# Values turned to token rows at the end of their projection, the bonus per token and head, in one layer of a hybrid backbone

## The chip, the cores and the metric

The kernel runs on one core of a Trainium2 chip, as one launch. The metric is the device time of a run in microseconds. Three runs of the kernel before took 1710.25 to 1720.92 us, median 1714.06; the profiled execution took 1717.3, and its trace spans 1715.5.

## The reference

One layer: 512 latent tokens and 256 context tokens of width 2048 are normalised, modulated and projected by one input matrix. Group A (16 heads of 64) is a state recurrence in two directions; each direction starts from the final state of the context's scan. Group B (16 query heads on 4 key heads) is windowed attention with all context keys. Both are gated, and projected by one output matrix. The part that the change is about:

```python
def _rwkv_output(y, prep, r_k, ln_g, ln_b):
    r, v, _, _, _, kd = prep
    mu = jnp.mean(y, axis=-1, keepdims=True)
    var = jnp.mean(jnp.square(y - mu), axis=-1, keepdims=True)
    yn = ((y - mu) * lax.rsqrt(var + GN_EPS)).reshape(B, L, RWKV_WIDTH) * ln_g + ln_b
    bonus = jnp.einsum('blhn,bldhn,hn->blh', r, kd, r_k)[..., None] * v
    return yn + bonus.reshape(B, L, RWKV_WIDTH)
```

The bonus is one number for each token and head, times that token's 64 values of the head; `kd` is summed over the two directions. `v` is also what the recurrence writes into its state, and there it is wanted with tokens on partitions; `r`, `k` and the normalised output are worked on with channels on partitions.

## The kernel before

Everything is float32. The large products (input and output projection) are split in three float32r products of high and low halves. A weight part (128 input rows times 4, 128 columns) is loaded to a tile `wf`, halved by ScalarE and VectorE to `whi` and `wlo`, and used by 12 matmuls with 512 columns. These are called filler here.

No instruction is issued where the program text stands. The text is recorded as a list of operations with their dependences; `order` (line 430) plays them through with a duration for each and writes one fixed sequence per engine: operations of the recurrence and attention go by the length of the path behind them, and filler products go where no such operation is ready. All are then issued by line 497, which is why every row of the profile has that line; tiles tell operations apart. A tile name stands for a slot in a ring of buffers, which several tensors share: `kv` holds keys and values of a pair, `g` scratch, `p` the tensors of a latent pair and of its output (`r`, `kds`, `bv`, `h`), `uv` the values in token rows in the scan, `kon` constants (identity, the ones of the heads).

The stages, with their times in the trace:

- 0 to 226 us: normalisation and the first eight column tiles of the projection together (`lockstep`), among them the values of pairs 0, 1 and 2.
- 226 to 690: eight context units (segment 0), one for each pair of heads, with 14 further column tiles as filler, of 512 latent and 256 context columns each. The latent accumulators are two banks (`pl`), the context accumulator one (`pc`).
- 650 to 1361: eight pairs, each with two latent units (segments 1 and 2, the two directions). A unit goes through `pair` (once for both), `prep`, `stacks`, `relay_out`, `solve`, `levels` and `scan`; the second unit ends in `rwkv_out`, which normalises, adds the bonus, gates and stores `dmix`. Filler are the remaining input tiles (receptance, gates, queries), and then the first quarter of the output projection.
- 1280 to 1414: norms and rotary of queries and keys; the last input tiles. The loads of `dmix` into `xl`, `q` and `rz` serve the output projection.
- 1414 to 1580: attention, with output projection as filler; then output projection alone to the end.

Of the values, `evac` (985) stores a projected column tile by channel to `dv`. `pair` (1039) loads it to `kv`, turns it by two or four transposes (`pv`, in a bank of the ring `pt`), copies it to a `g` slot and stores it as token rows to `vt`; `scan` loads it from there to `uv`. The bonus is made in `stacks` (1158): `rr = r * r_k * kds`, then one product with a block of ones, 128x512, which gives each channel the sum of its head, then VectorE's product with the values of `kv` into `bv`. `bv` has one buffer; it takes the normalised output in `rwkv_out` (1379), is gated in place and is the source of the store of `dmix`. `h` is a ring of two.

Of the kernel before, what the change touches and what calls it, by code (L numbers as in the profile page):

```python
# [16 lines left out]
ALU = mybir.AluOpType  # L17
# [5 lines left out]
L = 512  # L23
C = 256
T = L + C
# [34 lines left out]
NLOCK = 4  # L60
# [114 lines left out]
s ssq:8 rsq0:8 rsq1:8 gmu:8 gvar:8 rso0:8 rso1:8 pc:8*4 sc4:8 ms4:16 xtmp:80 smid:128 mf:128 invx:128 ur:128 sm:128*2  # L175
"""
CTX = BOTH + """
x xi:256*2 qt:256 wga:512 | kv k:256 v:256 kk:256 | kr0 kr:1024 | kr1 kr:1024 | kr2 sh:768 gsel:4 | kk gsum:512
# [7 lines left out]
kv k:512 v:512 | kk kk:512 | p r:512 kds:512 bv:512 h:512*2 | sh sh:512  # L186
# [323 lines left out]
class Body:  # L510
# [61 lines left out]
    def setup(self):  # L572
        nc, a = self.nc, self.a
# [8 lines left out]
        o = 0  # L582
        c = constants()
# [13 lines left out]
        v = nc.vector  # L597
# [7 lines left out]
        d = self.dram  # L605
        self.dk = [self.t(d, (128, T), f"dk{p}") for p in range(8)]
        self.dv = [self.t(d, (128, T), f"dv{p}") for p in range(8)]
# [144 lines left out]
    def lockstep(self):  # L752
        nc, a = self.nc, self.a
        lp = self.lp = self.pool(LOCK)
# [18 lines left out]
        ada, mod, xs, wts, raw = {}, {}, {}, {}, []  # L773
        accl = [self.t(pp, (128, 512), f"accl{j}") for j in range(NLOCK)]
        accc = [self.t(pp, (128, 512), f"accc{j}") for j in range(NLOCK // 2)]
        accc = [accc[j // 2][:, 256 * (j % 2):256 * (j % 2) + 256] for j in range(NLOCK)]
# [127 lines left out]
        for c in range(2 * KC):  # L904
# [16 lines left out]
            if c == KC - 1:  # L921
                for j in range(NLOCK):
                    x = self.t(lp, (128, T), "raw")
# [8 lines left out]
        for j in range(NLOCK):  # L932
            for i in range(2):
                nc.tensor.matmul(pb[:, 4 * j + 2 * i:4 * j + 2 * i + 2], lhsT=acb[i][:, 128 * j:128 * j + 128],
                                 rhs=ones, start=True, stop=True)
        nc.vector.tensor_copy(bias.rearrange("p j i -> p (j i)"), pb[:, ::2])
        for j, x in enumerate(raw):
            for i, (o, n, *_) in enumerate(streams):
                nc.scalar.activation(x[:, o:o + n], x[:, o:o + n], AF.Identity, bias=bias[:, j, i:i + 1])
            self.evac(NLOCK + j, x[:, :L], x[:, L:], self.t(lp, (128, T), "xs"))  # L940
# [44 lines left out]
    def evac(self, j, pl, pc, o=None):  # L985
        nc = self.nc
        kind, i, _ = COLS[j]
# [27 lines left out]
        dst = {"k": self.dk, "v": self.dv, "ak": self.dak, "av": self.dav, "q": self.dq, "r": self.dr,  # L1015
               "zr": self.dzr, "za": self.dza}[kind][i]
        n = T if pc is not None else L
# [21 lines left out]
    def pair(self, s, p, wk, ps, lat):  # L1039
        nc = self.nc  # L1040
        n, off = (L, 0) if lat else (C, L)
        ntt = n // 128
# [4 lines left out]
        s.v = self.t(wk, (128, n), "v")  # L1047
        nc.sync.dma_start(out=s.v, in_=self.dv[p][:, off:off + n])
        self.n += 1
        s.vt = self.t(self.dram, (n, 128), f"vt{self.n}")  # L1050
# [24 lines left out]
        pv = self.t(ps, (128, 512), "pt", nm="pv")[:, :n]  # L1075
        for t in range(ntt):
            nc.tensor.transpose(pv[:, 128 * t:128 * t + 128], s.v[:, 128 * t:128 * t + 128], self.ident)
        vt = gen("vt")[:, :n]
        nc.scalar.copy(vt, pv)
        nc.sync.dma_start(out=s.vt.rearrange("(t q) c -> q t c", q=128), in_=vt.rearrange("q (t c) -> q t c", c=128))  # L1080
# [77 lines left out]
    def stacks(self, s, wk, ps):  # L1158
# [43 lines left out]
        if seg == 2:  # L1202
            rr = self.t(wk, (128, 512), "g", nm="rr")
            nc.vector.scalar_tensor_tensor(rr, pr.r, self.par["r_k"][:, p:p + 1], pr.kds, ALU.mult, ALU.mult)
            pb_ = pt("pbon")
            nc.tensor.matmul(pb_, lhsT=self.kon["bones"], rhs=rr, start=True, stop=True)
            pr.bv = self.t(wk, (128, 512), "bv")
            nc.vector.tensor_tensor(pr.bv, pb_, pr.v, ALU.mult)
# [170 lines left out]
    def rwkv_out(self, p, s, wk, ps):  # L1379

        nc = self.nc
        gen = lambda nm: self.t(wk, (128, 512), "h", bufs=2, nm=nm)
# [20 lines left out]
        nc.gpsimd.tensor_tensor(s.bv, o, s.bv, ALU.add)  # L1403
        o = s.bv
        self.gate(o, self.dzr[p], gen("gz"), gen("gth"))
# [296 lines left out]
```

## Time and profile before

| | |
|---|---|
| median of three runs | 1714.06 us (1710.25 to 1720.92) |
| profiled execution | 1717.3 us |
| its span | 1715.5 us |
| TensorE busy | 1570.0 us, 92% |
| weight loads busy | 1213.2 us, 71% |
| VectorE busy | 1342.5 us, 78% |
| ScalarE, GpSimd busy | 705.5 and 403.9 us |
| moved by DMA | 232.99 MB, mean 136 GB/s |
| mean granted clock of TensorE | 0.97 |

Times count from the start of the span. PE is TensorE, PEld its weight loads, DVE VectorE, ACT ScalarE, POOL GpSimd, SPq the queue of DMA issues. Matmuls overlap one another, so the busy times of single ones add up to more than the time that they take; the distance between two starts is what one costs. "Clock" is the share of full speed that TensorE was granted. A wait is put down to the releaser that came last.

### The profile page before, as it was taken

Reading aid. Unit: us, or ns where it says so; the run is one execution under the profiler, and the core shown is the slowest. Engines: PE = TensorE matmul, PEld = TensorE weight load, DVE = VectorE, ACT = ScalarE, POOL = GpSimd, SP = SyncE. Lnnn points to the kernel's source line nnn. Section 1 sums busy time; section 2 is a strip of 40 time slices with the busy share of each in tenths; the row PEclk is TensorE's granted clock in tenths of the full one; section 3 lists DMA queues with packets and bytes.
Section 4 is the critical chain, followed back from the end, with each engine's and each line's share of the span. In section 5 each row is a group of like instructions: output and inputs, shape, how many; then the busy total and the mean of one; then the engine's idle time right before and its main releaser. Section 6 shows DMA issues by size and latency. Waiting matters only on the chain.

```text
span 1715.5 us, 34198 instructions
## 1 busy us (share of the span) xinstructions
PE 1570.0 (92%) x12374; PEld 1213.2 (71%) x12374; DVE 1342.5 (78%) x3913; ACT 705.5 (41%) x1460; POOL 403.9 (24%) x615
## 2 busy tenths in 40 slices
PE   7998888999999999988899999899988979999998
PEld 4666777776777777766676676667765658787886
DVE  2457888887989646878789778887888877989965
ACT  3432363333334223433343334343433437777733
POOL 2358621110111002122223121222223350202000
PEclk9999999999999999989999999999998999999999
DMA  9976465534545433433343334243433363122136
GB/s 348 325 252 209 129 185 153 148 103 136 156 132 167 143 112 122 129 84 111 89 128 99 109 99 132 78 118 95 125 105 110 120 203 115 64 67 68 50 124 189
DMA packets 218122, 232.99 MB, mean 136 GB/s; under 512 B 79584, under 2 KB 140384, under 8 KB 217952
## 3 DMA queue, kind: packets, MB, share of 16 engines
q1 hardware_dynamic: 217952, 230.80, 43.7%
q8 instruction: 97, 1.59, 0.4%
q14 instruction: 73, 0.60, 0.1%
HBM read 194.55 MB, written 36.18 MB: 134 GB/s over the span
## 4 chain that ended last, share of the span: by engine, by line
PE 29%; DVE 23%; DMA 7%; issue 3%; ACT 1%; SPq 1%; POOL 0%; DVEq 0%; ACTq 0%; POOLq 0%
PE psum L497 29%; DVE x L497 7%; DVE s L497 5%; DVE e L497 2%; DMA x<-iw 2%; DVE ar L497 2%; DVE wlo.1_45_339 L497 2%; DVE wlo.0_42_301 L497 1%; SPq L497 1%; DMA iw<-x 1%; DVE bk L497 1%; DVE p L497 1%; DVE uv L497 1%; DMA nb<-it 1%; DMA wf.0_40_246<-in_wo_dram 1%
## 5 line engine op out<-in xcount | busy, mean ns | idle before, releaser
L497 PE MATMUL psum<-xh,whi.0_41_297 128*128 128x512 f32 x624 | 244.9, 415 | 1.2 <-ACT xh L497 0.5
L497 PE MATMUL psum<-xh,whi.1_44_327 128*128 128x512 f32 x624 | 240.3, 408 | 0.7 <-ACT xh L497 0.7
L497 PE MATMUL psum<-xh,wlo.1_45_339 128*128 128x512 f32 x528 | 218.2, 413 | 5.7 <-DVE wlo.1_45_339 L497 5.7
L497 PE MATMUL psum<-xh,wlo.0_42_301 128*128 128x512 f32 x528 | 215.8, 409 | 2.6 <-DVE wlo.0_42_301 L497 2.6
L497 PE MATMUL psum<-xl,whi.0_41_297 128*128 128x512 f32 x432 | 178.1, 412 | 5.8 <-DVE xl L497 5.8
L497 PE MATMUL psum<-xl,whi.1_44_327 128*128 128x512 f32 x432 | 177.4, 411 | 0.7 <-DVE xl L497 0.6
L497 DVE TENSOR_TENSOR s<-x,nb 128x60 f32<-128x60 f32 (+21 forms) x648 | 158.5, 245 | 10.0
L497 DVE TENSOR_TENSOR x<-x,s 128x60 f32<-128x60 f32 (+21 forms) x648 | 155.4, 240 | 10.6
L497 PEld LDWEIGHTS psum<-xh,whi.0_41_297 128*128 128x128 f32 x624 | 119.1, 193 | 30.1 <-issue 4.5
L497 PEld LDWEIGHTS psum<-xh,whi.1_44_327 128*128 128x128 f32 x624 | 118.7, 191 | 25.4 <-issue 2.3
L497 PEld LDWEIGHTS psum<-xh,wlo.1_45_339 128*128 128x128 f32 x528 | 101.7, 193 | 29.3 <-DVE wlo.1_45_339 L497 7.9
L497 PEld LDWEIGHTS psum<-xh,wlo.0_42_301 128*128 128x128 f32 x528 | 100.8, 191 | 25.7 <-DVE wlo.0_42_301 L497 4.2
L497 PEld LDWEIGHTS psum<-xl,whi.0_41_297 128*128 128x128 f32 x432 | 83.2, 193 | 26.1 <-DVE xl L497 7.5
L497 PEld LDWEIGHTS psum<-xl,whi.1_44_327 128*128 128x128 f32 x432 | 83.2, 193 | 17.9 <-DVE xl L497 1.5
L497 PE MATMUL psum<-kr,bk 64*128 64x128 f32 (+1 forms) x640 | 70.5, 305 | 20.1 <-DVE x L497 6.3
L497 PEld LDWEIGHTS psum<-kr,bk 64*128 64x128 f32 (+1 forms) x640 | 56.4, 201 | 36.8 <-issue 9.3
L497 ACT COPY uv<-psum 64x128 f32<-64x128 f32 (+2 forms) x103 | 28.9, 280 | 127.2 <-PE psum L497 64.3
L497 ACT ACTIVATE e<-psum,drv 128x256 f32<-128x256 f32 x96 | 44.6, 473 | 84.6 <-PE psum L497 33.2
L497 PE MATMUL psum<-uv,kb 128*64 128x64 f32 (+1 forms) x848 | 65.5, 248 | 10.6 <-DVE uv L497 10.5
L497 PEld LDWEIGHTS psum<-uv,kb 128*64 128x64 f32 (+1 forms) x848 | 47.1, 145 | 39.3 <-DVE uv L497 16.5
L497 POOL TENSOR_TENSOR s<-s 128x128 f32<-128x128 f32 x56 | 32.5, 580 | 173.3 <-DVE s L497 149.5
L497 PE MATMUL psum<-uv,ar 64*64 64x64 f32 (+1 forms) x1280 | 71.6, 238 | 1.8 <-DVE uv L497 1.3
(375 smaller groups left out, 3829.3 us busy)
## 6 DMA issues: line engine op xcount, KB each, us to landing
wf.0_40_246<-in_wt_dram SPq DMA_DIRECT2D x72, 256.0 KB, 2.9
wf.1_43_252<-in_wt_dram SPq DMA_DIRECT2D x72, 256.0 KB, 2.9
wf.2_50_264<-in_wt_dram SPq DMA_DIRECT2D x72, 256.0 KB, 2.8
x<-in_wga_dram SPq DMA_DIRECT2D x64, 256.0 KB, 2.8
nb<-it SPq DMA_DIRECT2D x24, 496.0 KB, 3.9
kr<-in_wss_dram SPq DMA_DIRECT2D x22, 512.0 KB, 5.7
kb<-in_wss_dram SPq DMA_DIRECT2D x22, 512.0 KB, 6.0
uv<-vt SPq DMA_DIRECT2D x48, 128.0 KB, 3.1
```

The source lines that it names most:

```text
L497: getattr(getattr(self.nc, o.eng), o.f)(*a, **k)
```

## The change

The column tiles of values are turned where their projection ends (`evac`): transposes into the tile's own accumulators, copies back, and two stores of token rows to `dvt`. `dv`, `vt`, the loads, transposes and stores in `pair` go, and `scan` loads from `dvt`. The bonus becomes four products with two columns (one number for each token and head, `bon`, 128x8, two buffers). In `rwkv_out` the values are loaded as token rows into a slot of `h` (now a ring of three), multiplied by `bon` on GpSimd, turned by four transposes into a bank of the ring `pu`, and added by VectorE to the normalised output, which is then gated. `bv` and the slot for the values in `kv` are gone.

```diff
@@ -172,10 +172,10 @@
 """
 BOTH = """
 g g:512 | wzh wzh:512 | wzl wzl:512 | bk bk:1024 | nb nb:992 | e th0:256 th1:256 en:260 ez:260
-s ssq:8 rsq0:8 rsq1:8 gmu:8 gvar:8 rso0:8 rso1:8 pc:8*4 sc4:8 ms4:16 xtmp:80 smid:128 mf:128 invx:128 ur:128 sm:128*2
+s ssq:8 rsq0:8 rsq1:8 gmu:8 gvar:8 rso0:8 rso1:8 pc:8*4 sc4:8 ms4:16 xtmp:80 smid:128 mf:128 invx:128 ur:128 sm:128*2 bon:8*2
 """
 CTX = BOTH + """
-x xi:256*2 qt:256 wga:512 | kv k:256 v:256 kk:256 | kr0 kr:1024 | kr1 kr:1024 | kr2 sh:768 gsel:4 | kk gsum:512
+x xi:256*2 qt:256 wga:512 | kv k:256 kk:256 | kr0 kr:1024 | kr1 kr:1024 | kr2 sh:768 gsel:4 | kk gsum:512
 ar0 ar:1024*2 | kb0 kb:1024 | kb1 kb:1024 | uv0 uv:1024 | uv1 uv:1024
 """
 XCTX = """
@@ -183,7 +183,7 @@
 """
 LAT = BOTH + """
 x xi:256*2 qt:256 mb:256*2
-kv k:512 v:512 | kk kk:512 | p r:512 kds:512 bv:512 h:512*2 | sh sh:512
+kv k:512 | kk kk:512 | p r:512 kds:512 h:512*3 | sh sh:512
 kr2 kr:1024 | kr0 kr:1024 | kr1 kr:1024 | ar1 ar:2048 | ar2 ar:2048 | ar0 ar:2048
 kb2 kb:1024 | kb0 kb:1024 | kb1 kb:1024 | uv2 uv:1024 | uv0 uv:1024 | uv1 uv:1024
 """
@@ -604,7 +604,7 @@
         v.tensor_scalar(self.hw0, self.par["w0"], 0.5, None, ALU.mult)
         d = self.dram
         self.dk = [self.t(d, (128, T), f"dk{p}") for p in range(8)]
-        self.dv = [self.t(d, (128, T), f"dv{p}") for p in range(8)]
+        self.dvt = [self.t(d, (T, 128), f"dvt{p}") for p in range(8)]
         self.dak = [self.t(d, (128, T), f"dak{p}") for p in range(2)]
         self.dav = [self.t(d, (128, T), f"dav{p}") for p in range(2)]
         self.dmix = [self.t(d, (128, L), f"dmix{p}") for p in range(16)]
@@ -937,7 +937,7 @@
         for j, x in enumerate(raw):
             for i, (o, n, *_) in enumerate(streams):
                 nc.scalar.activation(x[:, o:o + n], x[:, o:o + n], AF.Identity, bias=bias[:, j, i:i + 1])
-            self.evac(NLOCK + j, x[:, :L], x[:, L:], self.t(lp, (128, T), "xs"))
+            self.evac(NLOCK + j, x[:, :L], x[:, L:], self.t(lp, (128, T), "xs"), (accl[j], accc[j]))
 
     def mms(self, pl, pc, hi, lo, kc, cstart=None):
         nc = self.nc
@@ -982,7 +982,7 @@
                   lambda acc, ws, first, last: self.products(*acc, ws),
                   lambda j, acc: self.evac(j, *acc))
 
-    def evac(self, j, pl, pc, o=None):
+    def evac(self, j, pl, pc, o=None, banks=None):
         nc = self.nc
         kind, i, _ = COLS[j]
         segs = [(pl, 0, L)] + ([(pc, L, C)] if pc is not None else [])
@@ -1012,7 +1012,17 @@
                     nc.scalar.copy(st, w[:, sl])
                     nc.vector.tensor_tensor(st[64:128], w[64:128, sl], st[64:128].bitcast(F32), ALU.subtract)
             return
-        dst = {"k": self.dk, "v": self.dv, "ak": self.dak, "av": self.dav, "q": self.dq, "r": self.dr,
+        if kind == "v":
+            fill, nc.fill = nc.fill, False
+            for p, (s, n) in zip(banks or (pl, pc), ((0, L), (L, C))):
+                for t in range(0, n, 128):
+                    nc.tensor.transpose(p[:, t:t + 128], o[:, s + t:s + t + 128], self.ident)
+                nc.scalar.copy(o[:, s:s + n], p[:, :n])
+                nc.sync.dma_start(out=self.dvt[i][s:s + n].rearrange("(t q) c -> q t c", q=128),
+                                  in_=o[:, s:s + n].rearrange("q (t c) -> q t c", c=128))
+            nc.fill = fill
+            return
+        dst = {"k": self.dk, "ak": self.dak, "av": self.dav, "q": self.dq, "r": self.dr,
                "zr": self.dzr, "za": self.dza}[kind][i]
         n = T if pc is not None else L
         nc.sync.dma_start(out=dst, in_=o[:, :n])
@@ -1044,10 +1054,7 @@
         s.lat, s.n, s.off = lat, n, off
         s.k = self.t(wk, (128, n), "k")
         nc.sync.dma_start(out=s.k, in_=self.dk[p][:, off:off + n])
-        s.v = self.t(wk, (128, n), "v")
-        nc.sync.dma_start(out=s.v, in_=self.dv[p][:, off:off + n])
-        self.n += 1
-        s.vt = self.t(self.dram, (n, 128), f"vt{self.n}")
+        s.vt = self.dvt[p][off:off + n]
         if lat:
             s.r = self.t(wk, (128, n), "r")
             nc.sync.dma_start(out=s.r, in_=self.dr[p])
@@ -1072,12 +1079,6 @@
         nc.vector.tensor_reduce(ssq, pn[:, :n].rearrange("p (m c) -> p m c", c=64), AX.X, ALU.add)
         nc.vector.tensor_scalar(ssq, ssq, 1e-24, None, ALU.max)
         inv = self.rsqrt(wk, ssq, 2 * ntt)
-        pv = self.t(ps, (128, 512), "pt", nm="pv")[:, :n]
-        for t in range(ntt):
-            nc.tensor.transpose(pv[:, 128 * t:128 * t + 128], s.v[:, 128 * t:128 * t + 128], self.ident)
-        vt = gen("vt")[:, :n]
-        nc.scalar.copy(vt, pv)
-        nc.sync.dma_start(out=s.vt.rearrange("(t q) c -> q t c", q=128), in_=vt.rearrange("q (t c) -> q t c", c=128))
         s.kk = self.t(wk, (128, n), "kk")
         pk = self.t(ps, (128, 512), "pt", nm="pinv")
         for t in range(ntt):
@@ -1203,9 +1204,11 @@
             rr = self.t(wk, (128, 512), "g", nm="rr")
             nc.vector.scalar_tensor_tensor(rr, pr.r, self.par["r_k"][:, p:p + 1], pr.kds, ALU.mult, ALU.mult)
             pb_ = pt("pbon")
-            nc.tensor.matmul(pb_, lhsT=self.kon["bones"], rhs=rr, start=True, stop=True)
-            pr.bv = self.t(wk, (128, 512), "bv")
-            nc.vector.tensor_tensor(pr.bv, pb_, pr.v, ALU.mult)
+            for t in range(4):
+                nc.tensor.matmul(pb_[:, 2 * t:2 * t + 2], lhsT=rr[:, 128 * t:128 * t + 128], rhs=self.sel2, start=True,
+                                 stop=True)
+            pr.bon = self.t(wk, (128, 8), "bon")
+            nc.vector.tensor_copy(pr.bon, pb_[:, :8])
 
     def relay_out(self, s, wk):
 
@@ -1379,7 +1382,7 @@
     def rwkv_out(self, p, s, wk, ps):
 
         nc = self.nc
-        gen = lambda nm: self.t(wk, (128, 512), "h", bufs=2, nm=nm)
+        gen = lambda nm: self.t(wk, (128, 512), "h", nm=nm)
         g = lambda x: x.rearrange("p (g v) -> p g v", g=8)
         bc = lambda x: x.unsqueeze(2).to_broadcast([128, 8, 64])
         py = s.py
@@ -1400,9 +1403,14 @@
             nc.tensor.transpose(pt[:, 128 * t:128 * t + 128], yc[:, 128 * t:128 * t + 128], self.ident)
         o = gen("go")
         nc.scalar.activation(o, pt, AF.Identity, scale=self.par["ln_g"][:, p:p + 1], bias=self.par["ln_b"][:, p:p + 1])
-        nc.gpsimd.tensor_tensor(s.bv, o, s.bv, ALU.add)
-        o = s.bv
-        self.gate(o, self.dzr[p], gen("gz"), gen("gth"))
+        v = gen("bv")
+        nc.sync.dma_start(out=v.rearrange("q (t c) -> q t c", c=128), in_=s.vt.rearrange("(t q) c -> q t c", q=128))
+        nc.gpsimd.tensor_tensor(g(v), g(v), bc(s.bon), ALU.mult)
+        pt = self.t(ps, (128, 512), "pu", nm="pbt")
+        for t in range(4):
+            nc.tensor.transpose(pt[:, 128 * t:128 * t + 128], v[:, 128 * t:128 * t + 128], self.ident)
+        nc.vector.tensor_tensor(o, o, pt, ALU.add)
+        self.gate(o, self.dzr[p], v, gen("gth"))
         nc.sync.dma_start(out=self.dmix[p], in_=o)
 
     def gate(self, o, dz, z, th):
```

The order of work moves with it. The queue of DMA issues (SP) at the store of pair 7's output, before; `in_wt` is the input weights, `in_wo` the output weights, `dqf` the queries:

```order
L497 DMA wf.0_40_246<-in_wo_dram 128x512
L497 DMA dza_143<-sh_6255 128x512
L497 DMA dqf_107<-p_6140 128x512
L497 DMA wf.1_43_252<-in_wo_dram 128x512
L497 DMA sh_6255<-dza_136 128x512
L497 DMA kv_220<-dqf_104 64x512
L497 DMA dqf_108<-bk_260 128x512
L497 DMA kv_220<-dqf_104 64x512 x2
L497 DMA dmix_91<-p_6140 128x512
L497 DMA wf.2_50_264<-in_wo_dram 128x512
L497 DMA q_1163<-dmix_90 128x512
L497 DMA kv_220<-dqf_104 64x512
```

and after the change, the store being the first row:

```order
L497 DMA dmix_91<-p_6237 128x512
L497 DMA wf.2_50_248<-in_wt_dram 128x512
L497 DMA wf.0_40_230<-in_wt_dram 128x512
L497 DMA wf.1_43_236<-in_wt_dram 128x512
L497 DMA dza_141<-sh_6266 128x512
L497 DMA wf.2_50_248<-in_wt_dram 128x512
L497 DMA wf.0_40_230<-in_wt_dram 128x512
L497 DMA wf.1_43_236<-in_wt_dram 128x512
L497 DMA wf.2_50_248<-in_wt_dram 128x512
L497 DMA dza_142<-sh_6266 128x512
L497 DMA wf.0_40_230<-in_wo_dram 128x512
L497 DMA wf.1_43_236<-in_wo_dram 128x512
```

Before, the store stood among loads of output weights. Now seven loads of input weights come between it and the first of those; the first load of `dmix` into `xl` is the next row.

The same queue at the store of pair 1's output, before; `dv_75` is the values of pair 3, `nb` belongs to a unit's solve:

```order
L497 DMA wf.2_50_264<-in_wt_dram 128x512
L497 DMA wf.0_40_246<-in_wt_dram 128x512
L497 DMA wf.1_43_252<-in_wt_dram 128x512
L497 DMA dmix_85<-p_6140 128x512
L497 DMA dr_125<-sh_6255 128x512
L497 DMA wf.2_50_264<-in_wt_dram 128x512
L497 DMA kv_220<-dv_75 128x512
L497 DMA wf.0_40_246<-in_wt_dram 128x512
L497 DMA nb_1146<-it_189 128x1x992
L497 DMA iw_188<-x_1030 32x8x32 x3
```

and now; `dvt_73` is the values of pair 1, `dzr_129` its gate:

```order
L497 DMA dr_125<-sh_6266 128x512
L497 DMA wf.2_50_248<-in_wt_dram 128x512
L497 DMA p_6237<-dvt_73 128x4x128
L497 DMA wf.0_40_230<-in_wt_dram 128x512
L497 DMA wf.1_43_236<-in_wt_dram 128x512
L497 DMA p_6237<-dzr_129 128x512
L497 DMA dzr_133<-sh_6266 128x512
L497 DMA wf.2_50_248<-in_wt_dram 128x512
L497 DMA dmix_85<-p_6237 128x512
L497 DMA wf.0_40_230<-in_wt_dram 128x512
L497 DMA it_180<-ar_77_6371 32x8x32 x2
```

The load of a later pair's values right behind the store is gone; in front of the store are now the loads of the pair's own values and, behind those, of its gate.

Counted over the whole order: from one pair's `nb` loads to the next, 10 to 11 and 16 to 17 weight parts in turn were issued before, and about 11.3 evenly now. At the last product of the scans 3572 filler products stood ahead on TensorE, and now 3417; at the first attention score 3722 and now 3707; behind the last score 294 and now 309. Between the last product of the scans and the first score TensorE has 150 filler products among 191 rows before, and 290 among 323 now.

## Rows read from the trace of the kernel before

**Rows 1.** The page's busy time, share of the span and instructions by engine, whole span.
```profile
PE 1570.0 (92%) x12374; PEld 1213.2 (71%) x12374; DVE 1342.5 (78%) x3913; ACT 705.5 (41%) x1460; POOL 403.9 (24%) x615
```

**Rows 2.** Stretches: length, busy us (instructions) by engine, TensorE clock, DMA share, GB/s.
```profile
240.00:690.00 450.00, 420.53 (x3424) 336.72 (x3423) 354.66 (x1146) 159.95 (x340) 59.35 (x126) 0.98 0.47 139
690.00:1300.00 610.00, 556.10 (x5151) 411.70 (x5151) 511.35 (x1753) 228.51 (x482) 150.13 (x309) 0.97 0.37 107
1580.00:1715.50 135.50, 129.24 (x710) 107.48 (x708) 94.58 (x178) 64.31 (x133) 3.98 (x4) 0.98 0.39 119
1361.20:1414.50 53.30, 45.04 (x196) 33.80 (x194) 44.56 (x116) 22.37 (x39) 28.97 (x16) 0.90 0.58 185
```

**Rows 3.** Timeline of TensorE at a bonus product: start, us, instruction, how many.
```profile
855.51 0.40 PE L497 MATMUL psum<-xh,wlo.1_45_339 128*128 128x512 f32 x1
...
856.21 1.02 PE L497 MATMUL psum<-g,kon 128*128 128x512 f32 x2
857.07 0.60 PE L497 MATMUL psum<-kon,bk 128*128 128x128 f32 x4
857.42 0.48 PE L497 MATMUL psum<-xh,wlo.1_45_339 128*128 128x512 f32 x1
857.74 0.40 PE L497 MATMUL psum<-xh,whi.1_44_327 128*128 128x512 f32 x1
```

**Rows 4.** Waits of TensorE, 690 to 1300 us: releaser, us, times, longest.
```profile
PE psum L497 <- DVE x L497: 19.7, 18, 3.2
PE psum L497 <- DVE s L497: 9.6, 17, 1.3
...
PE psum L497 <- DMA kv<-dv: 0.9, 2, 0.6
```

**Rows 5.** Stretches from one store of `dmix` to the next, columns as in rows 2.
```profile
799.50:870.10 70.60, 64.89 (x592) 48.54 (x591) 56.53 (x168) 27.35 (x57) 21.40 (x44) 0.98 0.32 94
870.10:968.70 98.60, 89.83 (x856) 66.15 (x855) 88.43 (x321) 37.36 (x80) 21.66 (x44) 0.98 0.39 114
968.70:1039.40 70.70, 66.24 (x601) 49.42 (x601) 54.75 (x155) 27.38 (x56) 20.91 (x44) 1.00 0.36 108
1039.40:1139.60 100.20, 90.82 (x843) 66.53 (x842) 83.79 (x308) 35.87 (x78) 20.14 (x44) 0.93 0.37 108
1139.60:1208.00 68.40, 64.19 (x583) 47.69 (x583) 54.69 (x161) 25.80 (x54) 22.00 (x44) 0.95 0.33 96
1208.00:1311.20 103.20, 91.23 (x866) 67.28 (x865) 92.56 (x366) 39.49 (x83) 26.86 (x49) 0.98 0.38 111
```

**Rows 6.** Timeline of VectorE and SP's queue, 870 to 875 us.
```profile
870.09 0.33 SPq L497 DMA_DIRECT2D dmix<-p  x1
...
874.17 0.69 DVE L497 TENSOR_TENSOR p<-psum,kv 128x512 f32<-128x512 f32 x1 [1.30 <-DMA dmix<-p]
...
874.89 0.32 SPq L497 DMA_DIRECT2D kv<-dv  x1
```

**Rows 7.** Timeline of TensorE, products of two columns (eight such rows).
```profile
221.58 0.28 PE L497 MATMUL psum<-s,ar 128*128 128x2 f32 x2
...
223.28 0.48 PE L497 MATMUL psum<-xh,whi.0_41_297 128*128 128x512 f32 x1
```

**Rows 8.** Groups by line and form: count, busy us, mean ns, idle before.
```profile
L497 PE MATMUL psum<-kon,p 128*128 128x128 f32 x360 | 53.2, 279 | 3.6 <-POOL p L497 2.2 <-DVE p L497 1.2 <-DVE kb L497 0.2
...
L497 DVE TENSOR_TENSOR p<-psum,kv 128x512 f32<-128x512 f32 x8 | 5.5, 686 | 1.3 <-DMA dmix<-p 1.3
...
L497 POOL TENSOR_TENSOR p<-p,s 128x512 f32<-128x512 f32 x8 | 8.7, 1092 | 82.4 <-DVE s L497 44.6 <-ACT s L497 14.7 <-ACT whi.0_41_297 L497 13.8
...
L497 ACT COPY kb<-psum 128x512 f32<-128x512 f32 x48 | 27.0, 587 | 51.8 <-PE psum L497 49.6 <-DVE s L497 0.8 <-DVE wlo.0_42_301 L497 0.7
```

**Rows 9.** Timeline of SP's queue, 1396 to 1402.5 us.
```profile
1396.56 5.87 SPq L497 DMA_DIRECT2D kv<-dqf  x2
```

**Rows 10.** DMA issues: count, KB each, median us from issue to landing.
```profile
uv<-vt SPq DMA_DIRECT2D x48, 128.0 KB, 3.1
```

## The prediction

> **What bounds the kernel now.** I read the busy line first, then the stage windows, single matmuls, the waits and the latent phase pair by pair. TensorE is busy for 92% of the span, VectorE for 78% [rows 1]. By stage the picture is sharper [rows 2]: in the last 135.5 us TensorE is busy for 129.2, while in the latent phase (690 to 1300) it is busy for 556.1 of 610 and VectorE for 511.4. Filler matmuls of 128x512 start at 855.51 and, three steps on, at 856.21: one every 0.233 us, though each has 0.40 beside it [rows 3]. So a matmul's duration is not its cost; its spacing is. What TensorE waits for in the latent phase is VectorE above all: 19.7 us for the tile `x` and 9.6 for `s` [rows 4], both of the solve.
>
> Cut at the stores of `dmix`, that phase has a limp [rows 5]: pairs take 70.6, 98.6, 70.7, 100.2, 68.4 and 103.2 us. I count as lost what TensorE is idle, and its busy time times the missing clock: 5.7 + 1.3 = 7.0 us in the first row, 8.8 + 1.8 = 10.6 in the second, and so on; 18.9 in the three short rows (9.0% of 209.7, VectorE busy 79%), 40.1 in the long ones (13.3% of 302.0, VectorE 88%), 59.0 of 511.7 in all.
>
> One reason for the limp stands in one place [rows 6]: at 870.09 the store of pair p's output is issued, only 4.08 us later VectorE may write the next pair's bonus (it had waited 1.30 us for that store, since the one buffer `bv` is the store's source), and 0.72 us later the values of the pair after are loaded, since the product had read the buffer they come into. One pair's end gates the start of the pair after next.
>
> **The change, part by part.** All sums go against the profiled execution, 1717.3 us; it is 3.2 above the median of 1714.06.
>
> *TensorE, bonus.* Out goes one 128x512 product in two passes a pair: 0.86 us from its start to the next instruction's (856.21 to 857.07) [rows 3]. In come four 128x2 products, eight passes; sixteen such passes took 221.58 to 223.28, 0.106 each [rows 7], so eight take 0.85. Even. New are four transposes a pair, 32 in all. Four in a row hold the next filler product off by 0.35, and that one its own successor by 0.09 more than the usual 0.23 [rows 3]: 0.44 x 8 = 3.5. The bounds are 0.106 for each (3.4) and the 279 ns with latency of the group's row [rows 8], 8.9. I take **+3.5**, the row in which filler stands on both sides.
>
> *TensorE, values.* 48 transposes go from the units into the ends of eight projection tiles. Same count, same shape: 0. Away goes the wait for `kv<-dv`, 0.9 us in the latent phase [rows 4]: **-0.9**. But the accumulators of a values tile are now held until its transposes and copies are through. Where the next tile wants the single context bank at once, six tiles would pay about 1.5 us each (0.35 of transposes, a copy out of PSUM of up to 0.59 for each stream [rows 8]), up to 9; in the order six filler products on another bank stand between the two groups of transposes, and more behind them, so I take **+0.5**, near the lower end of 0. The context stage has 29.5 idle us in 450 [rows 2], into which such a wait may fall as well.
>
> *VectorE, GpSimd.* Eight products with PSUM (0.686 [rows 8]) become eight adds with PSUM of the same shape: even. Eight 128x8 copies come in, a sixty-fourth of that size each; even at 0.686 they are 5.5 beside 1342.5 busy, and as small as they are I put 0. GpSimd gives eight adds for eight products of the same shape, 404 busy in all [rows 1]: 0.
>
> *Transfers.* 16 fewer on SP's queue and 4 MB less; TensorE's waits for DMA in the latent phase are that 0.9. 0.
>
> *The order.* This moves most. With the chain of rows 6 gone the pairs come evenly: about 11.3 weight parts are issued from one pair to the next, against 10 to 11 and 16 to 17 in turn before. At the last scan step TensorE has 155 filler products fewer behind it than before. At 0.233 that is 36.1 us earlier, if TensorE stays the bound. They don't vanish: between that point and the first attention score stand 290 filler products, against 150, since attention may not start before the last projection tile. That stretch was 53.3 us long, with 45.0 busy at a clock of 0.90, 40.5 of work, so 12.8 lost [rows 2]; the work is 150 x 0.233 = 35.0 and 5.5 for 41 other rows. Its end went by the store of pair 7, which stands on SP's queue right behind a load for the norms that held the queue for 5.87 us from 1396.56 [rows 9]. The order now has the store in front of seven loads of input weights, so 290 x 0.233 + 3.6 (33 other rows, fewer than the 41 above) = 71.2 of work covers it, and I leave 6 lost, about the middle between nothing and 12.8: 77.2. So the first score stands 36.1 earlier, 23.9 later: -12.2; after the last score 15 products more are left: +3.5. Together **-8.7**.
>
> *The denser chain.* The same chain in six pairs of 475.6 instead of 511.7 us leaves VectorE less slack: 430.8 busy less 13 weight parts (155 / 12) of one 128x512 operation at 0.69 each is 422, 88.7% of the time. By the long rows (13.3% lost at 88%, 0.48 points more for each point) 65.6 are lost, +6.6. By the mean of all rows (11.5%), since an even load is like neither half, 54.8, -4.3. Nothing shows an even cadence, so I take the middle: **+1.2**.
>
> Sum: 3.5 - 0.9 + 0.5 - 8.7 + 1.2 = **-4.4**, that is 1712.9 for such an execution and **1710** on the median. All that is gained is fewer idle microseconds; the work of TensorE, which sets the end, is the same.
>
> **The rivals.** *The limp was the loss* (faster): an even chain loses as little as the short rows do, 9.0% of 475.6 = 43 instead of 59, -16 where I put +1.2: -21.6, **1692**. For it: the short rows have the same engines and the same mix. Against: they have VectorE at 79%, and 89% is what comes.
>
> *TensorE has slack* (faster): if the weight loads, busy 71% [rows 1], were the measure of TensorE, the filler behind the chain would be taken in its gaps, and the whole 36.1 come off: -36.1 + 3.5 - 0.9 + 0.5 = -33.0, **1681**. Against it: in the last 135.5 us, filler alone, weight loads are busy 107.5, 79%, with TensorE busy for 129.2 [rows 2]; that is this kernel's ceiling, and 71 of 79 is near it. The Trainium skill, "Perfetto Trace Analysis", section "Identifying the Most-Contended Engine", calls matmul busy time a bad measure of how near a kernel is to the roofline and the busy share of weight loads a good one; by that rule a fifth to a quarter of TensorE would be free. The trace agrees on the first half only.
>
> *VectorE becomes the bound* (slower): the chain doesn't shorten, because each pair needs some 70 us of VectorE (422 / 6) and its operations queue behind those of the next pair. If six pairs still take 511.7, the 36.1 aren't won while the filler behind them has to be done all the same: -4.4 + 36.1 = +31.7, **1746**; half of it, +13.7, is 1728. It decides by cadence: I forecast 79.3 us a pair, no gain is left from 80.0, a per cent is lost from 82.9. For it: VectorE is at 90% in the second and the last of rows 5 already, and TensorE waits for it [rows 4]. Against: in those two rows TensorE still is busy for 91 and 88%.
>
> *The output step holds the chain* (slower): per pair the values are now loaded after the buffer of the centred output is free, some 3.1 us as for the same rows now [rows 10], then multiplied (1.09 [rows 8]), turned (0.44) and added (0.69): 5.3 us in which a bank of the `pu` ring, on which the next pair's stacks wait, is given back later. Seven times 5.3 = 37 at most, on -4.4 that is +33, **1747**. Against: the ring has two banks and now serves 13 uses a pair instead of 12. That the change doesn't do what it says (values ready earlier, and yet no pair starts earlier, since something else held it) has the price of the VectorE rival.
>
> **How the numbers follow.** A per cent, 17 us, is what a measurement of this kernel can tell from no change. Chances: the forecast, anything within a per cent, 0.49; the limp 0.22; slack 0.07; VectorE the bound, past the point where a per cent is lost, 0.15; output step 0.07. So faster 0.29, same 0.49, slower 0.22. The range leaves out the slack rival and the upper half of the slower ones: 1686 (the limp's 1692 with nothing lost at the transition, -6) to 1737 (VectorE, beyond its half way).
>
> **What would show it.** Right: the stores of `dmix` 76 to 83 us apart, evenly; no wait of the bonus for `dmix<-p`; TensorE busy about 93% of the six pairs' time less clock; from the last scan step to the first score 74 to 80 us, filler at 0.23 us in it; first score 5 to 15 us earlier than 1414.5; the tail as before. The limp: under 8 us lost a pair. VectorE: the cadence at 83 or more with VectorE over 92%, waits for `x` and `s` well above 30 us. The output step: idle time of TensorE ended by `p` or by the `pu` bank. Wrong altogether: a context stage that ends more than 9 us later, or a wait for the stores of turned values ahead of the first unit.

## The result

The changed kernel took 1689.11 us (median of four runs, 1683.97 to 1695.99) where the kernel before took 1715.72 beside it: a ratio of 0.985, interval 0.981 to 0.989. In a second set of runs (below) it was 0.988 (0.986 to 0.990). So it is 20 to 27 us faster. The profiled execution is the fastest of the four, 1683.97 us.

The profile after, first its line of busy times, which answers to [rows 1]:

```profile
PE 1554.4 (92%) x12454; PEld 1207.8 (72%) x12454; DVE 1332.7 (79%) x3921; ACT 705.6 (42%) x1460; POOL 394.8 (23%) x615
```

The shares have hardly moved: 92% TensorE, 72% weight loads, 79% VectorE. The shares of a span can't tell where 34 us of span went. The stages can. Columns as in [rows 2]; first the kernel before, cut at 226 and 690 us, at the first and the seventh store of `dmix` and at the first attention score:

```profile
226.00:690.00 464.00, 432.10 (x3476) 346.55 (x3475) 365.18 (x1177) 168.87 (x359) 60.76 (x128) 0.97 0.48 142
690.00:799.50 109.50, 97.73 (x875) 72.48 (x874) 91.80 (x329) 38.76 (x82) 22.22 (x45) 0.94 0.36 104
799.50:1311.20 511.70, 467.21 (x4333) 345.62 (x4332) 430.76 (x1474) 193.24 (x407) 132.97 (x269) 0.97 0.36 106
1311.20:1414.50 103.30, 87.47 (x624) 64.07 (x622) 83.52 (x273) 38.55 (x72) 44.05 (x35) 0.91 0.51 159
1414.50:1715.50 301.00, 286.14 (x1682) 238.86 (x1682) 239.91 (x459) 183.76 (x394) 28.61 (x20) 0.98 0.31 97
```

and the changed kernel, cut at the same events:

```profile
226.00:690.00 464.00, 439.42 (x3554) 353.39 (x3553) 375.83 (x1213) 175.75 (x373) 61.70 (x129) 0.99 0.48 140
690.00:794.10 104.10, 95.02 (x876) 71.24 (x874) 92.98 (x318) 41.91 (x91) 25.25 (x56) 0.98 0.36 106
794.10:1253.05 458.95, 415.04 (x4192) 310.08 (x4189) 406.08 (x1459) 176.43 (x374) 126.05 (x260) 0.98 0.37 106
1253.05:1383.00 129.95, 117.42 (x754) 88.59 (x753) 88.41 (x272) 44.92 (x80) 36.60 (x32) 0.96 0.49 153
1383.00:1681.80 298.80, 287.00 (x1698) 238.42 (x1696) 236.53 (x459) 183.56 (x395) 28.09 (x20) 1.00 0.31 97
```

Lost time, counted as in the prediction (the stretch less TensorE's busy time times its clock), comes out of each row: 464 - 432.10 x 0.97 = 44.9 in the first. The table has that for the traces of before and after and for a second trace of each kernel, taken later. The clock in a row is rounded to 0.01; summed over stretches of 2 us, every figure of the table comes out within 3 us:

| lost, us | before | again | after | again |
|---|---|---|---|---|
| first 226 us | 26.7 | 31.4 | 27.6 | 29.0 |
| context stage, 226 to 690 | 44.9 | 49.3 | 29.0 | 31.0 |
| 690 to the first store of `dmix` | 17.6 | 15.9 | 11.1 | 14.0 |
| six pairs | 58.5 | 54.7 | 52.2 | 57.2 |
| seventh store to first score | 23.7 | 23.4 | 17.2 | 17.3 |
| first score to the end | 20.6 | 16.6 | 11.8 | 11.6 |

The largest part is one that the prediction had at +0.5: the context stage, 14 to 20 us less. The stretch ahead of the first store of `dmix` gives 2 to 7, the end of the latent phase 6 to 7, the rest of the program 5 to 9, the first 226 us and the six pairs nothing that both traces bear out.

Part of it is clock, part idleness. With the whole span cut in stretches of 2 us, the trace of before has 20 places where the granted clock is below full, which miss 44.5 us of work between them; the second trace 26 places and 51.4. After has 12 and 24.3, and 16 and 29.0. Over all runs the mean granted clock was 0.970 before and 0.980 after; within 29 runs of the kernel before (the two longest of 31 left out) the time went with it, some 11 us for each 0.01.

The pairs, which answer to [rows 5]:

```profile
794.10:871.90 77.80, 72.45 (x729) 54.71 (x725) 67.77 (x238) 29.14 (x63) 21.84 (x45) 0.96 0.35 104
871.90:954.30 82.40, 74.86 (x744) 55.86 (x742) 74.27 (x251) 31.09 (x66) 20.41 (x45) 1.00 0.37 105
954.30:1025.70 71.40, 64.78 (x671) 48.26 (x666) 63.76 (x232) 29.19 (x62) 19.56 (x44) 1.00 0.38 111
1025.70:1099.60 73.90, 69.84 (x698) 51.66 (x696) 64.11 (x230) 28.76 (x62) 20.89 (x45) 0.95 0.35 102
1099.60:1177.20 77.60, 69.42 (x712) 52.45 (x710) 67.95 (x240) 28.73 (x62) 20.14 (x44) 0.98 0.35 103
1177.20:1253.00 75.80, 63.65 (x652) 47.09 (x652) 68.17 (x273) 29.51 (x60) 23.16 (x39) 0.96 0.39 111
```

The limp is gone: 71 to 82 us a pair instead of 70 and 100 in turn, 458.9 for six where 511.7 were. VectorE is busy for 88% of that stretch.

### The profile page after: what moved, and what is told of

It reads as the page before. It is cut to its first block, busy times and chain, and to the rows that moved or that the text cites. A ratio compares the mean times of both kernels' runs of the same rounds, so it can differ in the third digit from the quotient of the medians.

```text
span 1681.8 us, 34358 instructions
## 1 busy us (share of the span) xinstructions
PE 1554.4 (92%) x12454; PEld 1207.8 (72%) x12454; DVE 1332.7 (79%) x3921; ACT 705.6 (42%) x1460; POOL 394.8 (23%) x615
## 5 line engine op out<-in xcount | busy, mean ns | idle before, releaser
L497 DVE TENSOR_TENSOR x<-x,s 128x60 f32<-128x60 f32 (+21 forms) x648 | 159.2, 246 | 10.1
L497 PEld LDWEIGHTS psum<-xl,whi.0_41_281 128*128 128x128 f32 x432 | 82.2, 190 | 23.7 <-DVE xl L497 5.9
L497 PE MATMUL psum<-kr,bk 64*128 64x128 f32 (+1 forms) x640 | 65.7, 294 | 12.6 <-DVE x L497 5.4
L497 PEld LDWEIGHTS psum<-kr,bk 64*128 64x128 f32 (+1 forms) x640 | 52.7, 191 | 28.8 <-issue 8.8
L497 PEld LDWEIGHTS psum<-uv,kb 128*64 128x64 f32 (+1 forms) x848 | 46.8, 143 | 32.5 <-DVE uv L497 15.9
```

The costliest lines, as they stand in the source:

```text
L497: getattr(getattr(self.nc, o.eng), o.f)(*a, **k)
```

## The experiments

Each ran beside the kernel before on one chip, and its ratio is to that. "Limp" is the turn of short and long pairs.

**Half of the change, the bonus.** The kernel before with the bonus as the change has it (`stacks` and `rwkv_out`), values turned in the units and stored to `vt` as before:

```diff
-kv k:512 v:512 | kk kk:512 | p r:512 kds:512 bv:512 h:512*2 | sh sh:512
+kv k:512 v:512 | kk kk:512 | p r:512 kds:512 h:512*3 | sh sh:512
...
-            nc.tensor.matmul(pb_, lhsT=self.kon["bones"], rhs=rr, start=True, stop=True)
-            pr.bv = self.t(wk, (128, 512), "bv")
-            nc.vector.tensor_tensor(pr.bv, pb_, pr.v, ALU.mult)
+            for t in range(4):
+                nc.tensor.matmul(pb_[:, 2 * t:2 * t + 2], lhsT=rr[:, 128 * t:128 * t + 128], rhs=self.sel2, start=True,
+                                 stop=True)
+            pr.bon = self.t(wk, (128, 8), "bon")
+            nc.vector.tensor_copy(pr.bon, pb_[:, :8])
```

> Half of the change: the bonus per token and head, added through transposes in the output step; values still stored by channel, turned in each unit. In its order the pairs come evenly, as in the changed kernel. Theory A (two sources: the limp of the latent phase with what follows it, some 18 us of lost TensorE time in the traces, and the context stage, some 16): 8 to 18 us under the kernel before, the context stage as before (lost time near 45 us between 226 and 690). Rival B (the limp is all): 22 to 28 us under. Rival C (values at the projection's end are all): within 5 us of before.

0.999 (0.996 to 1.003), so nothing. A and B missed; C held here, but falls with the run of the values below, from which it wanted 20 to 28 us and which gave 10. The limp is gone in its trace (stores 72 to 83 us apart), and the end of the latent phase loses 15.1 instead of 23.7. It is given back where the pairs are:

```profile
811.50:1285.50 474.00, 429.35 (x4199) 322.17 (x4196) 404.46 (x1451) 180.25 (x381) 126.61 (x259) 0.95 0.38 108
```

474 - 429.35 x 0.95 = 66.1 us lost, against 58.5 before in a stretch 37.7 longer.

**The buffer alone.**

```diff
-kv k:512 v:512 | kk kk:512 | p r:512 kds:512 bv:512 h:512*2 | sh sh:512
+kv k:512 v:512 | kk kk:512 | p r:512 kds:512 bv:512*2 h:512*2 | sh sh:512
```

> The kernel before with one edit: two buffers for the bonus product, so that the next pair's product need not wait for the store of the output. In its order the pairs come evenly. Theory A and rival B both: the same gain as the run of the bonus alone, less the 3.5 us of its 32 transposes, so 11 to 21 us under before (A) or 25 to 31 (B); stores of dmix 72 to 82 us apart. Rival D (the bonus's new form itself, not the buffer, makes the gain): within 5 us of before.

0.997 (0.993 to 1.000); stores 75 to 83 us apart. One more buffer takes the limp away, as the wait in [rows 6] said, and again the pairs lose more (64.0) for it. So the limp was real, its cause was the one that the rows showed, and it cost some 5 us, which the interval hardly tells from nothing. A and B wanted 11 us or more, which only the end of the interval reaches.

**The other half, the values.** Values turned where their projection ends, `scan` loads from `dvt`; for the bonus of the latent pairs `dv` is stored and loaded as well. Part of the edit, against the changed kernel (not shown: the bonus goes back to its form before):

```diff
+            nc.sync.dma_start(out=self.dv[i], in_=o[:, :L])
             for p, (s, n) in zip(banks or (pl, pc), ((0, L), (L, C))):
...
         s.vt = self.dvt[p][off:off + n]
+        if lat:
+            s.v = self.t(wk, (128, n), "v")
+            nc.sync.dma_start(out=s.v, in_=self.dv[p])
```

> The other half: values turned where their projection ends and loaded by the scans as token rows; they are stored by channel as well, for the bonus of the latent pairs, which stays as before. In its order the limp stays. Theory A: 8 to 16 us under before, lost TensorE time between 226 and 690 near 29 us instead of 45, pairs still in turn near 70 and 100 us. Rival B: within 5 us. Rival C: 20 to 28 us under.

0.994 (0.990 to 0.998), 10 us: in A's span, but not at A's place, the context stage:

```profile
226.00:690.00 464.00, 432.63 (x3505) 347.88 (x3504) 370.21 (x1181) 173.55 (x371) 64.51 (x128) 0.97 0.49 143
```

464 - 432.63 x 0.97 = 44.3 lost (39.4 when summed over stretches of 2 us), where A wanted 29.

**The values of the context units alone.** As before in the latent units; only the 256 context columns are turned at the projection's end (part of the edit):

```diff
+            p = (banks or (pl, pc))[1]
+            for t in range(0, C, 128):
+                nc.tensor.transpose(p[:, t:t + 128], o[:, L + t:L + t + 128], self.ident)
+            nc.scalar.copy(o[:, L:], p[:, :C])
+            nc.sync.dma_start(out=self.dvt[i].rearrange("(t q) c -> q t c", q=128),
+                              in_=o[:, L:].rearrange("q (t c) -> q t c", c=128))
```

> Values turned at the projection's end for the context units alone; latent units as before. Theory A: as the run of the values alone, within 5 us of it, since the latent units' own turning costs only some 2 us of waits (8 to 16 us under before). Rival B: within 5 us of before.

0.994 (0.990 to 0.997), 11 us, and here at the place:

```profile
226.00:690.00 464.00, 436.40 (x3534) 351.54 (x3533) 376.80 (x1221) 173.79 (x370) 68.51 (x131) 0.99 0.49 142
```

464 - 436.40 x 0.99 = 32.0 lost in the context stage, as after (29.0 and 31.0). The first store of `dmix` stands at 780.78, the earliest of all traces. What it wins there it too gives back in part in the pairs: 517.9 - 473.17 x 0.95 = 68.4. Why the run of all the values has no such gain in the context stage isn't settled. It stores by channel out of the tile into which it then copies the turned values; ScalarE waits for that store twice in the stage, 3.5 us in all (here once, 2.6), which is too little, and no run takes the rest apart.

**The changed kernel again.**

> The changed kernel once more, beside the runs below. If its gain stands: 20 to 30 us under before, mean granted clock about 0.980 where before has 0.970. A second trace tells which of its stretches at half clock stand in the order (same places, within 15 us) and which are chance: theory A (places set by the order) expects two thirds of the twelve again, theory N (chance) fewer than half.

0.988 (0.986 to 0.990), 20 to 21 us, at the lower edge of what was expected, with the clock at 0.981. Nine of the twelve places of lower clock stand again within 15 us, and two more 18 us later (the whole trace is 12 us later from 1250 on). Of the twenty of before, seventeen stood again in its second trace, which has eight more elsewhere. Most places belong to the order.

**Both halves, the bonus in its old form.** The kernel of the values' half, with `bv:512*2`:

> Values turned at the projection's end (by channel stored as well), and the bonus by channel as before but with two buffers: both halves of the change without the bonus's new form. In its order the pairs come evenly. If the two effects are what counts and the halves reinforce each other: 18 to 28 us under before, as the changed kernel. If they only add (values 10, buffers 5): 12 to 18 under. If the bonus's new form is what makes the rest: 5 to 12 under.

0.990 (0.987 to 0.992), 18 us, on the border of the first two cases: 10 and 5 added make 16. The new form of the bonus is worth at most the few us between this and the changed kernel, and the intervals overlap.

**Other orders of the same two kernels.**

```diff
-TICK, COLMIN, FWAIT, FB, LOOK, GRP = 3413, 4000, 0, 80000, 30, 5
+TICK, COLMIN, FWAIT, FB, LOOK, GRP = 3413, 4000, 0, 80000, 36, 5
```

> The changed kernel with one number of the planner moved (LOOK 30 to 36): the cadence of the pairs stays, but a third of TensorE's instructions stand at other places. Theory A (even pairs and shorter context units are the gain): within 6 us of the changed kernel, so 18 to 30 under before. Theory L (the particular order is lucky: fewer stretches at half clock by chance of where filler falls): 8 us or more slower than the changed kernel, clock back at 0.970 to 0.975.

> The kernel before with the same number moved; its limp stays, a fifth of TensorE's instructions stand elsewhere. Theory A: within 6 us of the kernel before. Theory L: it moves by 8 us or more either way.

The changed kernel: 0.985 (0.983 to 0.987), clock 0.980. The kernel before: 0.996 (0.994 to 0.997), clock 0.971, 7 us, a little over what A allowed. So another order can be worth some 7 us, and the change's 20 to 27 are more than that. One other order of two kernels is all that was run, though, and every edit here moves the order: the 5, 10 and 11 us of the runs above are hardly told apart from it.

**A second buffer for the scratch tile.** `g` has one buffer. What waits for it I had not read: the queue that issues the DMAs. Waits of SP's queue in the trace of before, columns as in [rows 4], the first rows and one further down:

```profile
SPq L497 <- DVE s L497: 277.0, 164, 11.1
SPq L497 <- DVE x L497: 259.7, 114, 9.9
...
SPq L497 <- DMA vt<-g: 16.7, 8, 3.1
```

Eight times, 16.7 us in all, the queue stood until a store of turned values had landed; seven of these, 14.6 us, lie in the context stage, where the next issue was the load of the next weights into `g`. One such place, SP's queue from 292 to 302 us:

```profile
292.00 0.39 SPq L497 DMA_DIRECT2D vt<-g  x1
292.44 0.47 SPq L497 DMA_DIRECT2D wf.0_40_246<-in_wt_dram  x1
295.29 1.15 SPq L497 DMA_DIRECT2D g<-in_wz_dram  x2
296.55 0.53 SPq L497 DMA_DIRECT2D x<-in_wga_dram  x1
...
301.47 0.57 SPq L497 DMA_DIRECT2D nb<-it  x1
```

The store goes out at 292.00, and the load into `g` at 295.29; the loads of `x` and `nb` stand behind it. After has no row of that wait. So:

```diff
-g g:512 | wzh wzh:512 | wzl wzl:512 | bk bk:1024 | nb nb:992 | e th0:256 th1:256 en:260 ez:260
+g g:512*2 | wzh wzh:512 | wzl wzl:512 | bk bk:1024 | nb nb:992 | e th0:256 th1:256 en:260 ez:260
```

> The kernel before with one edit: two buffers instead of one for the scratch tile g, which holds the weights wz, the squares, the turned values until their store has landed, and the bonus's operand. Theory G (the values' half gains because it takes the turned values and their store out of that one buffer): the values' gain without moving anything, 7 to 13 us under before. Theory P (it gains because the loads, transposes and copies themselves leave the units): within 4 us of before.

0.988 (0.983 to 0.994), 20 us: above G's span, and against P. The same place in its trace:

```profile
292.44 0.51 SPq L497 DMA_DIRECT2D g<-in_wz_dram  x1
...
293.63 0.43 SPq L497 DMA_DIRECT2D vt<-g  x1
294.11 0.49 SPq L497 DMA_DIRECT2D g<-in_wz_dram  x1
...
296.50 0.33 SPq L497 DMA_DIRECT2D x<-in_wga_dram  x1
...
301.48 0.57 SPq L497 DMA_DIRECT2D nb<-it  x1
```

The load goes out ahead of the store. But what stood behind it is no earlier: `x` at 296.50 and `nb` at 301.48, where they were at 296.55 and 301.47. At this place the 3 us reached the loads into `g` and nothing that came after. Its pairs still limp (71.1 and 102.9 us the first two), which shows from the other side that the limp was not the loss. But it doesn't win where the change does:

```profile
226.00:690.00 464.00, 431.49 (x3483) 345.25 (x3484) 365.86 (x1179) 169.98 (x362) 62.81 (x129) 0.98 0.49 142
```

Its context stage loses 464 - 431.49 x 0.98 = 41.1, 4 to 8 us less than before where the change loses 14 to 20 less; the stretch before the first store of `dmix` loses 9.4, 6 to 8 less. The one buffer held up the kernel before; that the change frees it is shown for the wait on the queue, and not that the context stage gains by it.

**Two buffers for each.**

> The kernel before with both edits: two buffers for g and two for the bonus product, nothing else moved. Theory G: as the values by token rows with two bonus buffers, 14 to 22 us under before, so that buffers alone give most of the change's gain. Theory P: as two bonus buffers alone, 2 to 9 us under.

0.989 (0.985 to 0.994): within G's span, no more than `g` alone. Again even pairs add nothing by themselves.

**Two buffers in the changed kernel.**

> The changed kernel with two buffers for g. Theory G: g has lost its long holder, so within 5 us of the changed kernel (17 to 30 under before). Rival: g still holds up the units by wz, squares and the bonus's operand, 8 us or more under the changed kernel.

0.981 (0.977 to 0.986), median 1687.14: the lowest ratio of the study, and below both kernels in the tables above. From the changed kernel's first 0.985 it is not told apart; from its second 0.988 (0.986 to 0.990) it lies just clear, in other runs on another chip. At 32 us under before it is outside G's span, so whether `g` still holds the changed kernel by some us stays open.

**The kernel before, a second trace.**

> The kernel before, for a second trace. If its stretches at half clock are set by the order, at least two thirds of the twenty stand within 15 us of where they stood, lost time (idle and missing clock) is 180 to 195 us, and the one at 1500 us, in the attention, tells whether the 9 us by which the changed kernel's last 300 us lose less are the order's.

1715.55 us, lost time 191, seventeen of the twenty places again. That at 1500 isn't among them, and the last stretch lost 16.6, so of its 9 us some 3 to 4 were that one execution's.

## Why the prediction was right and wrong

The range held the time and the direction of the sum (-4.4) was right. The likeliest case, a change within a per cent, was not: it is 20 to 27 us, 1.2 to 1.5%. That the range reached so far down is luck: its lower end stands on the rival of the limp, whose mechanism the runs refute. Point by point:

*The work of TensorE* was sized right. Four bonus transposes before a filler product:

```profile
786.93 0.60 PE L497 MATMUL psum<-kon,p 128*128 128x128 f32 x4
787.29 0.48 PE L497 MATMUL psum<-xh,whi.0_41_281 128*128 128x512 f32 x1
787.60 0.40 PE L497 MATMUL psum<-xl,whi.0_41_281 128*128 128x512 f32 x1
```

0.36 to the filler, 0.08 more to the next, 0.44 as I had it; times eight 3.5. Span less all lost time (26.7 and 27.6 in the first 226 us) went from 1523.5 to 1532.9, though, by 9; summed over stretches of 2 us it is 5 (1525.5 to 1530.0), and 8 in the second traces. So the 3.5 fit, and some us beside them are unexplained.

*The other engines.* Their operations cost what the rows had said, within 3% (0.678 for 0.686, 1.117 for 1.092), and the small copies less than their bound:

```profile
L497 DVE TENSOR_TENSOR p<-p,psum 128x512 f32<-128x512 f32 x8 | 5.4, 678 | 2.9 <-PE psum L497 2.9
...
L497 DVE COPY s<-psum 128x8 f32<-128x8 f32 x9 | 1.4, 158 | 0.0
```

```profile
L497 POOL TENSOR_TENSOR p<-p,s 128x512 f32<-128x512 f32 x16 | 17.9, 1117 | 42.2 <-DVE s L497 25.9 <-issue 8.6 <-DVE ar L497 4.1
```

*The order* did what its rows said: even pairs, a full stretch of filler ahead of the first score, and from the seventh store to there 6 to 7 us less lost where I had 6.8 from the last scan step. This holds in every kernel with even pairs (15 to 19 us lost, 20 to 25 in those with the limp). The last product of the scans and the first score, before:

```profile
1364.08 0.70 PE L497 MATMUL psum<-uv,ar 128*64 128x64 f32 x8
...
1414.53 0.38 PE L497 MATMUL psum<-ar,kr 128*128 128x256 f32 x1 [0.76 <-ACT ar L497]
```

and after:

```profile
1303.73 0.45 PE L497 MATMUL psum<-uv,ar 128*64 128x64 f32 x8 [1.22 <-DVE uv L497]
...
1383.01 0.52 PE L497 MATMUL psum<-ar,kr 128*128 128x256 f32 x3
```

That stretch grew from 50.5 to 79.3 us, by 28.8 where I had 23.9 (51.0 to 79.3 in the second traces). But the scans end 60 us earlier (49 in the second traces) where I had 36.1, so the first score stands 31.5 us earlier (21.0), and not 5 to 15.

One reading in this part was wrong, though the sum hardly rests on it: the 5.87 us of [rows 9] are not one load that held the queue, but two, at 1396.56 and 1401.97, and in between the queue waits for GpSimd (waits of SP's queue from 1396 to 1403 us):

```profile
SPq L497 <- POOL kr L497: 4.9, 1, 4.9
```

*The denser chain.* VectorE at 88%, as forecast, and 52.2 and 57.2 us lost where I had 60.2. The rival that an even chain loses as little as the short rows gave 1692, which is nearly the time measured; as a mechanism it is refuted by three runs. Without the limp the kernel gained 0 and 5 us, and with the limp and a second `g` it gained 20. A rival's time can be met by another cause.

*The step that failed is that of the values and of the transfers.* I put 0 for 16 fewer issues and 0.9 for the wait for `kv<-dv`, since these were TensorE's waits for DMA. And for the context stage I looked at what the change adds there (accumulators held, +0.5, up to 9) and not at what it takes out of each of eight units in a row: load, two transposes, copy, store, load. The stage loses 14 to 20 us less, and the run on the context's values alone shows 13 to 17 of that. The added wait that I had bounded by 9 didn't show: TensorE's waits for DMA in the changed kernel name no `dvt` but for 0.4 us. The first unit is late (its load of `nb` goes out at 272.3, at 260.7 before), the eighth hardly (561.8 and 557.1).

How the removal shortens the stage stays open. A transfer can hold the queue without standing in TensorE's waits: the store out of `g` held it for 16.7 us. The kernels part by that wait:

| kernel | queue's wait for `vt<-g`, us | lost in the context stage | under before, us |
|---|---|---|---|
| before (and again) | 16.7 (15.3) | 44.9 (49.3) | |
| the bonus | 18.9 | 47.4 | 1 |
| two buffers for the bonus product | 13.5 | 50.5 | 5 |
| before, other order | 16.4 | 42.3 | 7 |
| the values | none | 44.3 | 10 |
| the context's values | 1.9 | 32.0 | 11 |
| the values, two bonus buffers | none | 43.6 | 18 |
| two buffers for `g` | 2.4 | 41.1 | 20 |
| two buffers for each | 4.2 | 47.8 | 18 |
| the change (and again) | none | 29.0 (31.0) | 25 (20) |
| the change, other order | none | 32.5 | 25 |
| the change, two buffers for `g` | none | 28.6 | 32 |

No kernel with the wait gained more than 7 us, and none without it, or with little of it, less than 10. But the context stage, where most of the wait lies, doesn't follow it: four kernels are rid of it or nearly so and still lose 41 to 48 there. That the queue held loads for VectorE's chain and TensorE then waited for VectorE is an argument, which the one place looked at doesn't bear out.

*The clock* was no term of my sum though it was in my count of losses. Between 15 and 27 of the microseconds that went are places of lower clock (44.5 and 51.4 before, 24.3 and 29.0 after). One that is left, in the changed kernel; TensorE idle for 2.21 us until VectorE's `s`, and the clock in the stretch ahead, behind and further on:

```profile
1273.82 0.45 PE L497 MATMUL psum<-s,q 64*64 64x64 f32 x8 [2.21 <-DVE s L497]
```

```profile
1266.00:1271.60 5.60, 5.39 (x74) 3.60 (x73) 5.50 (x24) 1.54 (x4) 2.47 (x6) 1.00 0.34 77
1273.80:1277.00 3.20, 3.18 (x60) 2.83 (x62) 2.11 (x8) 1.42 (x3) 1.39 (x2) 0.63 0.29 85
1278.00:1284.00 6.00, 5.86 (x61) 4.29 (x60) 2.64 (x8) 2.52 (x5) 1.33 (x3) 1.00 0.46 114
```

Full, 0.63 (part of it at the lower level of 1.2 GHz), and full again. So this idle stretch cost itself and then a part of what followed. Not every one does:

```profile
944.50 0.94 PE L497 MATMUL psum<-kr,bk 64*128 64x128 f32 x12 [1.88 <-DVE x L497]
```

Here the clock is 1.00 in the stretches of 2 us ahead (942 to 944) and behind (944 to 946).

*TensorE has slack* fell as a mechanism, though its 1681 is not far from the time measured: the filler behind the chain was not taken in gaps, for the stretch in which it stands grew by 28 to 29 us, and the last 132.8 us, filler alone, hold weight loads for 105.5, again 79%. The share of weight loads that the Trainium skill ("Perfetto Trace Analysis", "Identifying the Most-Contended Engine") takes for a measure thus stands at 79% here with filler alone, and reading it against 100% would have promised too much.

*VectorE becomes the bound* and *the output step holds the chain* did not come: six pairs took 76.5 us each (77.6 in the second trace). TensorE's waits for `p` grew to 7.9 us from VectorE and 3.2 from GpSimd in the whole span, from 1.9 and 2.2, so the second is there at a tenth of its price.

What stays open beside the context stage: the kernels with one part of the change give back in the pairs some of what they win elsewhere (66.1 us lost there with the bonus, 62.6 with the values, 68.4 with the context's values, 55 to 59 before, 52 to 60 in the kernels with the whole change), and a second `g` reaches nearly the change's gain by other stages. Why the pairs lose more with one part alone (hardly more with the values), no run here tells.

## What to carry to other kernels

Read the waits of the queue that issues the DMAs, and not only those of the busiest engine: a store out of a scratch tile with one buffer keeps that queue, when the next issue writes the tile, until it has landed, 2 us on the mean here, and TensorE's waits don't name it. What such a wait costs in the end is told by a run, not by its sum. An uneven rhythm of stages is not yet a loss; where filler can be done at any time, as here, evening it moved the filler and won little else. And try the buffer before the restructuring: one line (`g:512*2`) gave 20 us here, about as much as the whole change.

## What was not expected of the hardware

The stretches at lower clock come back at the same places from one execution to the next (seventeen of twenty, nine of twelve), each missing some 1.5 to 3.4 us of work (one 4.8); runs of one kernel still spread by over 1% (29 runs of before from 1704 to 1728, and two more at 1731 and 1733), with mean clocks of 0.961 to 0.977.
